# A11·B11 by seven quarter products as well, with partial sums kept in PSUM, one weight buffer for eight sums, and a new order of the groups

## The chip, the cores and the metric

The kernel runs on one core of a Trainium2 chip. The engines that matter are TensorE (PE in the profile; its weight loads are PEld), VectorE (DVE), ScalarE (ACT), GpSimd (POOL) and SyncE (SP), which here only issues DMAs. Each engine works through its own instructions in the order in which they were issued, and waits on semaphores for the others. SBUF is the on-chip memory that all engines use; PSUM holds the results of matmuls in eight banks of 128x512 f32, and here TensorE writes it, ScalarE and VectorE read it. The metric is device time in microseconds (us), the median of the runs shown. The kernel before takes 1509.22 us (three runs, 1507.74 to 1509.64).

## The reference

```python
def reference(x, w):                    # x: 8 x 2048 x 2048, w: 2048 x 2048, f32
    cs = np.cumsum(x, axis=1)
    diff = cs - np.concatenate([zeros, cs[:, :-1, :]], axis=1)
    return np.matmul(diff, w).astype(np.float32)
```

The difference of the running sum is x again, so what is computed is one product of a 16384x2048 matrix by a 2048x2048 matrix.

## The kernel before, in words

**Tiling.** x is cut into 128 row tiles of 128 rows. Tiles 0 to 3 are multiplied in bf16 while w arrives (`plain`). Tiles 4 to 7 are one group (`group_plain`), and the other 120 tiles are 30 groups of four (`group(g, ...)`, g = 8, 12, ..., 124). In a group the code calls the four tiles g, g+1, h = g+2 and h+1; `next_g`, `next_h`, `next_k`, `next_l` are the four tiles of the next group.

**Outer scheme.** w is cut into four blocks B11, B12, B21, B22 of 1024x1024, held in f16. T1 = B12-B11, T2 = B22-T1, T3 = B22-B12 and T4 = B21-T2 are made once. Row tiles g and g+1 give A11, A12 (the two halves of tile g along the contraction) and A21, A22 (those of tile g+1); h and h+1 give a second set. With S1 = A21+A22, S2 = S1-A11, S3 = A11-A21 and S4 = A12-S2, seven products replace eight: A11·B11, A12·B21, S4·B22, A22·T4, S1·T1, S2·T2, S3·T3. The four output blocks C11, C12, C21, C22 are sums of these. A product of one set is 16 matmuls of 128x512; for g and h together 32.

**Inner scheme.** A product for g and h together can itself be cut into quarters (two row tiles, two halves of the contraction, two column halves) and done by seven quarter products of four matmuls each, 28 instead of 32. It needs four sums of x parts (`sums_in`: s1 = a21+a22, s2 = s1-a11, s3 = a11-a21, s4 = a12-s2; VectorE, f16, 128x512 each) and four sums of weight parts (Q1 to Q4 of class `Inner`). The sums of weights are made once where there is room. Where there is not, the sum is made anew in every group into the one buffer `flow` (`passed` in the code): two such sets by GpSimd (`pass_fourth`, line 503), two by VectorE (lines 499 and 815), four instructions of 128x512 f16 a set. From g = 16 on (`five`) the products of A12, S4, A22 and S1 are done by sevens; A11·B11, S2·T2 and S3·T3 are whole. That makes 4x28 + 3x32 = 208 matmuls in a group.

**Evacuation.** Every quarter product ends in a PSUM bank of its own and is then added into the outputs it belongs to, in SBUF. The first part of an output is copied by ScalarE (`keep`, line 543, 16 of 128x512 a group), every other part is added by VectorE (`add`, line 546, out = bank x scale + out, all f32, 36 of 128x512 a group). An output half tile of 128x512 then goes to HBM (`put`, 16 DMAs of 256 KB a group, into seven rotating buffers).

**Input.** For each row tile SP loads two halves of 128x1024 f32 into `F` (`load`), ScalarE sums absolute values row by row (`weigh`, line 112), VectorE and GpSimd make the scale (`scale_of`), ScalarE writes the tile scaled in f16 into the first half's buffer (`narrow`, line 143), and two transposing DMAs bring it to the form that TensorE wants (`turn`). `F` has five half buffers: three for first halves, two for second halves. The transposed tile of the next group goes to the place of the same tile of this group, once that has been read for the last time.

**What sets the order.** Each engine's order is the order in which the code writes the instructions (`after` ties each to the one before on its engine), SP's queue of DMAs included. Nothing is planned by costs. The order of a group is written out by hand in `group`, with two-k steps of S2·T2 and S3·T3 (`go`, four matmuls each) put between the quarter products.

Of the kernel before, what the change touches and what calls it, by code (L numbers as in the profile page):

```python
# [10 lines left out]
def kernel(  # L11
# [51 lines left out]
    F = const.tile([P, 5, NH], f32, name="F")  # L63
# [6 lines left out]

    def bank(i):
        return psum.tile([P, NB], f32, name=f"b{i}")
# [14 lines left out]
    queue_of_x = [PLAIN, PLAIN + 2, PLAIN + 3]  # L87
    for t in range(PLAIN + 4, END, 4):
        queue_of_x += [t, t + 2, t + 1, t + 3]
    for i, t in enumerate(queue_of_x):  # L90
        where[t] = [F[:, i % 3, :], F[:, 3 + i % 2, :]]
# [4 lines left out]
    def load(t, i):  # L96
        if t < END:
            after(
                "sp",
                lambda: nc.sync.dma_start(  # L100
                    where[t][i], x2[ds(t * P, P), ds(i * NH, NH)]
                ),
            )
# [33 lines left out]
    def narrow(t, sides=range(2)):  # L137
        if t < END:
            s = scales[t]
            for i in sides:  # L140
                after(
                    "act",
                    lambda: nc.scalar.activation(  # L143
                        narrowed(t)[:, ds(i * NH, NH)], where[t][i], COPY, scale=s
                    ),
                )

# [3 lines left out]
    def turn(t, halves=range(2)):  # L151
        if t < END:
            for i in halves:
# [5 lines left out]
                )  # L159

    with tc.tile_pool(name="ring", bufs=7) as ring, tc.tile_pool(
        name="o", bufs=5
# [99 lines left out]
        def plain_out(h, r):  # L262
            for n in here(h, r):
                if h == r == 0:
                    c = F[:, 2, ds(n * NB, NB)]
                elif h == 0 or r > 0:
                    c = opool.tile([P, NB], f32, name="o")
                else:
                    c = ring.tile([P, NH], bf16, name="wb").bitcast(f32)
# [167 lines left out]
    class Quarter:  # L437
# [9 lines left out]
    spills = ctx.enter_context(  # L447
        tc.tile_pool(name="spills", bufs=1, space=bass.MemoryType.DRAM)
    )
    inner = inpool.tile([P, 24, NB], f16, name="inner")  # L450
    flow = inpool.tile([P, 4, NB], f16, name="flow")
    spill = [spills.tile([P, 4, NB], f16, name=f"spill{i}") for i in range(4)]
    spare = [inner[:, j, :] for j in range(8, 24)]
    spare += [B12[k][:, n, :] for k in range(KH) for n in range(2)]
    spare += [B22[k][:, 0, :] for k in range(4, 8)]
    spare.reverse()
    S1 = [Part(inner[:, ds(2 * i, 2), :]) for i in range(2)]
    passing = [Quarter(inner[:, j, :]) for j in range(4, 8)]
    free = [cpool.tile([P, NB], f32, name=f"c{i}") for i in range(7)]

    def pair():
        return [one_c() for _ in range(2)]

    def one_c():
        return free.pop(0)


    class Inner:
        def __init__(self, b):
            self.Q1, self.Q2 = ([spare.pop() for _ in range(4)] for _ in range(2))  # L470
            self.Q4 = None
            self.t11, self.t12, self.t21, self.t22 = (
                [t[:, n, :] for t in b[4 * a : 4 * a + 4]] for a in range(2) for n in range(2)
            )
            self.Q3 = self.t12

        def first(self):
            less(self.Q1, self.t12, self.t11)
            less(self.Q2, self.t22, self.Q1)

        def fourth(self):
            if self.Q4 is None:
                self.Q4 = [spare.pop() for _ in range(4)]
            less(self.Q4, self.t21, self.Q2)

        def third(self):
            less(self.t12, self.t22, self.t12)

    passed = [flow[:, k, :] for k in range(4)]

    def keep_flow(i):
        after("sp", lambda: nc.sync.dma_start(spill[i], flow))

    def bring_flow(i):
        after("sp", lambda: nc.sync.dma_start(flow, spill[i]))

    def less(dst, p, q):
        for k in range(len(dst)):
            after("dve", lambda: nc.vector.tensor_tensor(dst[k], p[k], q[k], SUB))  # L499

    def pass_fourth(i):
        for k in range(4):
            after("pool", lambda: nc.gpsimd.tensor_tensor(passed[k], i.t21[k], i.Q2[k], SUB))  # L503

    def total(dst, p, q, op):
        after("dve", lambda: nc.vector.tensor_tensor(dst.all, p.all, q.all, op))  # L506


    def steps(to, a, b, first, pieces):
        for i in range(pieces):  # L510
            ks = range(i * KH // pieces, (i + 1) * KH // pieces)

            def some():
                for k in ks:
                    for n in range(2):
                        said = nc.tensor.matmul(  # L516
                            to[n],
                            a[k],
                            b[k][:, n, :],
                            start=(first and k == 0),  # L520
                            stop=(k == KH - 1),
                            skip_group_check=True,
                        )
                return said

            yield lambda: after("pe", some)

    def product(to, a, b, first):
        for some in steps(to, a, b, first, 4):
            some()  # L530

    def quarter(to, a, b, first):
        def some():
            for k in range(4):
                said = nc.tensor.matmul(  # L535
                    to, a[k], b[k], start=(first and k == 0), stop=(k == 3), skip_group_check=True
# [5 lines left out]
    def keep(c, p, u):  # L542
        after("act", lambda: nc.scalar.activation(c, p, COPY, scale=u))  # L543

    def add(c, p, u):
        after("dve", lambda: nc.vector.scalar_tensor_tensor(c, p, u, c, MUL, ADD))  # L546

    def keeps(c, p, u):
        for n in range(2):
            keep(c[n], p[n], u)  # L550

    def adds(c, p, u):
        for n in range(2):
            add(c[n], p[n], u)

    def put(c, t, at):
        after("sp", lambda: nc.sync.dma_start(out2[ds(t * P, P), ds(at * NB, NB)], c))
        free.append(c)

    store = put  # L560

    def puts(c, t, h):
        for n in range(2):
            put(c[n], t, 2 * h + n)
# [4 lines left out]
    def sums_in(a, b, to):  # L569
        a11, a12, a21, a22 = a.half(0), a.half(1), b.half(0), b.half(1)  # L570
        s1, s2, s3, s4 = to

        def one():
            total(s1, a21, a22, ADD)
            total(s2, s1, a11, SUB)

        def two():
            total(s3, a11, a21, SUB)
            total(s4, a12, s2, SUB)

        return one, two, (a11, a12, a22, s1, s2, s3, s4)


    in_2, in_3 = Inner(B21), Inner(B22)
    in_3.Q4 = [spare.pop() for _ in range(4)]
    in_4, in_5 = Inner(T4), Inner(T1)
    for i in (in_2, in_4, in_5):
        i.Q4 = passed
    assert not spare

    def group_plain(g, X, Y, Z, V):
# [13 lines left out]
        C11g = pair()  # L605
        keeps(C11g, X, ug)
# [4 lines left out]
        adds(C11g, V, ug)  # L611
        puts(C11g, g, 0)
# [6 lines left out]
        C11h = pair()  # L619
        keeps(C11h, Y, uh)  # L620
# [7 lines left out]
        C22 = pair()  # L628
        keeps(C22, V, vg)
        total(S4g, A12g, S2g, SUB)  # L630
        product(X, S2g, T2, False)
        C12g = pair()
        keeps(C12g, X, ug)
# [13 lines left out]
        adds(C11h, Z, uh)  # L647
        puts(C11h, h, 0)
        adds(C12g, V, ug)
        puts(C12g, g, 1)  # L650
        product(Y, S2h, T2, False)
        C12h = pair()
        keeps(C12h, Y, uh)
        adds(C22, X, vg)
        puts(C22, g + 1, 1)
# [5 lines left out]
        C22 = pair()  # L661
        keeps(C22, Z, vh)
# [3 lines left out]
        in_2.first()  # L666
        in_2.fourth()
        load(h + 5, 0)
        load(h + 5, 1)
        keep_flow(0)  # L670
        scale_of(g + 5)
        adds(C22, Y, vh)
        puts(C22, h + 1, 1)
        product(Z, S4h, B22, False)
        in_2.third()
        adds(C12h, Z, uh)
        puts(C12h, h, 1)
        narrow(g + 5)
        turn(h + 4)
        product(X, A22g, T4, False)  # L680
        C21 = pair()
        keeps(C21, X, vg)
        puts(C21, g + 1, 0)
# [3 lines left out]
        in_3.first()  # L687
        in_3.fourth()
        in_3.third()
        product(Y, A22h, T4, False)  # L690
        C21 = pair()
        keeps(C21, Y, vh)
        puts(C21, h + 1, 0)
# [3 lines left out]
        turn(h + 5)  # L697


    def group(g, X, Y, q, e, v, w):  # L700
        h = g + 2
        five = g > PLAIN + 8
# [7 lines left out]
        next_g, next_h, next_k, next_l, then = g + 4, h + 4, g + 5, h + 5, g + 8  # L710
        P6g, P6h = steps(X, S2g, T2, False, 4), steps(Y, S2h, T2, False, 4)
        P7g, P7h = steps(X, S3g, T3, False, 4), steps(Y, S3h, T3, False, 4)

        def go(some, n=1):
            for _ in range(n):
                next(some)()

        def seven(A, Q, Cg, Ch, fill):
            a11, a12, a22, s1, s2, s3, s4 = A
            go(fill)  # L720
            quarter(q, a11, Q.t11, True)
            add(Cg[0], q, ug)
            quarter(e, s1, Q.Q1, True)
            add(Ch[1], e, uh)
            quarter(v, a12, Q.t21, True)
            add(Cg[0], v, ug)
            quarter(q, s2, Q.Q2, False)
            add(Cg[1], q, ug)
            quarter(e, s4, Q.t22, False)
# [281 lines left out]
```

## Time and profile before

| | before |
|---|---|
| median of three runs | 1509.22 us |
| the profiled execution, first to last instruction | 1507.4 us |
| its mean granted TensorE clock | 0.998 |
| one group, from the start of one A11·B11 to the next (1366.32 to 1411.70) | 45.38 us |
| TensorE busy in that group | 45.25 us |
| VectorE busy in that group | 40.97 us |
| ScalarE busy in that group | 26.55 us |
| GpSimd busy in that group | 11.17 us |

Busy times are unions of the instructions' spans, and the spans of neighbouring instructions overlap a little: a 128x512 add is 745 ns long, yet 18 in a row take 12.32 us. Where a price is wanted, the spacing of a row of equal instructions is the better number. "Idle before" is the time in which the engine did nothing before an instruction of the group, with what ended it.

### The profile page before, as it was taken

What the parts mean: (1) busy time and instruction counts of PE and PEld (TensorE: products, weight loads), DVE (VectorE), ACT (ScalarE), POOL (GpSimd) and SP (SyncE); (2) the same over time, 40 slices, a digit from 0 to 9 for tenths busy, and PEclk for the clock granted to TensorE, in tenths of its full rate; (3) what the DMA queues carried; (4) which work ended last, traced back from release to release, by engine and by line L of the source; (5) the groups of instructions that cost most, each with busy time, mean ns of one, the idle gap of its engine ahead of it and who ended that gap; (6) DMA issues with size and microseconds to landing.
All of it is one profiled execution on the core that took longest, in us unless ns stands there. A gap on an engine that the chain in (4) does not pass through costs nothing.

```text
span 1507.4 us, 21215 instructions
## 1 busy us (share of the span) xinstructions
PE 1480.5 (98%) x6799; PEld 661.8 (44%) x6799; DVE 1329.6 (88%) x2419; ACT 914.2 (61%) x1301; POOL 328.9 (22%) x360
## 2 busy tenths in 40 slices
PE   8988999999999999999999999999999999999998
PEld 3433444444444444444444444444444444444443
DVE  7987778889998899998899998999898899888997
ACT  5865656656656656656656656556656556666552
POOL 0100001122221122222122222122222122212222
PEclk9999999999999999999999999999999999999999
DMA  9988979988888988788987888987788988888962
GB/s 359 354 216 243 248 228 249 254 243 211 232 223 229 253 242 212 235 221 233 252 244 205 235 220 240 249 245 205 233 217 244 256 224 219 233 219 241 253 177 105
DMA packets 378912, 354.28 MB, mean 235 GB/s; under 512 B 274928, under 2 KB 275440, under 8 KB 378672
## 3 DMA queue, kind: packets, MB, share of 16 engines
q1 hardware_dynamic: 378240, 351.09, 83.5%
q0 software_dynamic: 560, 1.84, 0.3%
q8 instruction: 53, 0.87, 0.2%
q14 instruction: 59, 0.48, 0.1%
HBM read 151.52 MB, written 136.31 MB: 191 GB/s over the span
## 4 chain that ended last, share of the span: by engine, by line
PE 75%; DVE 13%; issue 4%; DMA 4%; ACT 3%; SPq 0%; DVEq 0%; ACTq 0%
PE b L535 37%; PE b L516 36%; DVE c L546 9%; DVE inner L506 3%; DMA W<-in_w_dram 2%; PE b L250 2%; ACT c L543 1%; DMA x<-F 1%; DVE W L499 1%; DMA W<-in_x_dram 0%; DMA out_dram<-c 0%; DVE x L506 0%; ACT W L361 0%; ACT waste L112 0%; DVE m L129 0%
## 5 line engine op out<-in xcount | busy, mean ns | idle before, releaser
L546 DVE SCALAR_TENSOR_TENSOR c<-b,u,c 128x512 f32<-128x512 f32 x1048 | 736.6, 745 | 125.4 <-PE b L535 81.3
L516 PE MATMUL b<-W,x 128*128 128x512 f16 x3072 | 717.9, 380 | 5.9 <-ACT c L543 3.8
L543 ACT ACTIVATE c<-b,u 128x512 f32<-128x512 f32 x496 | 315.5, 680 | 283.6 <-issue 147.8
L516 PEld LDWEIGHTS <-x 128*128 128x128 f16 x3072 | 300.9, 98 | 370.5 <-issue 8.4
L143 ACT ACTIVATE F<-F,s 128x1024 f16<-128x1024 f32 x246 | 282.4, 1148 | 162.3 <-DVE s L131 158.3
L535 PE MATMUL b<-W,inner 128*128 128x512 f16 x1392 | 338.3, 379 | 0.0
L112 ACT ACTIVATE waste<-F 128x1024 uint8<-128x1024 f32 x246 | 259.5, 1055 | 115.0 <-DMA F<-in_x_dram 110.9
L535 PEld LDWEIGHTS <-inner 128*128 128x128 f16 x1744 | 168.5, 98 | 215.3 <-DVE c L546 15.3
L132 POOL TENSOR_SCALAR u<-m,uw 128x1 f32<-128x1 f32 x124 | 66.6, 542 | 817.0 <-DVE m L129 809.0
L535 PEld LDWEIGHTS <-x 128*128 128x128 f16 x1560 | 152.1, 98 | 195.9 <-issue 14.6
L535 PE MATMUL b<-W,x 128*128 128x512 f16 x968 | 234.2, 379 | 1.5
L503 POOL TENSOR_TENSOR flow<-W 128x512 f16<-128x512 f16 x140 | 163.6, 1195 | 291.2 <-PE b L535 286.8
L506 DVE TENSOR_TENSOR x<-x,x 128x1024 f16<-128x1024 f16 (+1 forms) x214 | 147.2, 700 | 6.2 <-PE b L516 1.1
L503 POOL TENSOR_TENSOR flow<-W,W 128x512 f16<-128x512 f16 x84 | 94.9, 1160 | 0.0
L535 PE MATMUL b<-flow,x 128*128 128x512 f16 x352 | 90.3, 379 | 2.5 <-DVE c L546 2.5
L506 DVE TENSOR_TENSOR inner<-x,x 128x1024 f16<-128x1024 f16 (+1 forms) x122 | 67.4, 553 | 3.3 <-DMA x<-F 3.3
L250 PE MATMUL b<-wb,xP 128*128 128x512 bf16 x240 | 57.4, 393 | 5.0 <-ACT wb L234 3.6
L535 PE MATMUL b<-inner,x 128*128 128x512 f16 x240 | 61.6, 379 | 0.7 <-DVE x L506 0.7
L535 PE MATMUL b<-inner 128*128 128x512 f16 x240 | 61.6, 379 | 0.4 <-DVE c L546 0.4
L506 DVE TENSOR_TENSOR inner<-x,inner 128x512 f16<-128x512 f16 x60 | 51.7, 862 | 0.0
L112 ACT ACTIVATION_READ_ACCUMULATOR waste<-F 128x1 f32 x246 | 46.6, 190 | 0.0
L506 DVE TENSOR_TENSOR x<-inner,x 128x1024 f16<-128x1024 f16 x62 | 42.4, 683 | 3.2
(56 smaller groups left out, 510.2 us busy)
## 6 DMA issues: line engine op xcount, KB each, us to landing
out_dram<-c SPq DMA_DIRECT2D x496, 256.0 KB, 3.2
F<-in_x_dram SPq DMA_DIRECT2D x246, 512.0 KB, 4.9
W<-in_w_dram SPq DMA_DIRECT2D x32, 512.0 KB, 9.6
W<-in_x_dram SPq DMA_DIRECT2D x16, 256.0 KB, 7.7
x<-F SPq DMA_TRANSPOSE x246, 3.4
out_dram<-o SPq DMA_DIRECT2D x7, 256.0 KB, 3.6
spill<-flow SPq DMA_DIRECT2D x3, 512.0 KB, 2.6
out_dram<-o POOLq DMA_DIRECT2D x5, 256.0 KB, 4.2
```

Of the source, the lines that this page charges most:

```text
L112: lambda: nc.scalar.activation(waste, where[t][i], ABS, scale=1.0 / ROW, accum_out=sums_of[t][:, i : i + 1],),
L132: after("pool", lambda: nc.gpsimd.tensor_scalar(u, m, uw, None, MUL))
L143: lambda: nc.scalar.activation(narrowed(t)[:, ds(i * NH, NH)], where[t][i], COPY, scale=s),
L250: lambda: nc.tensor.matmul(ps[r][n], xP[:, r, ko, :], wb[h, ko][:, ds(n * NB, NB)], start=(ko == 0), stop=(ko == KO - 1),),
L499: after("dve", lambda: nc.vector.tensor_tensor(dst[k], p[k], q[k], SUB))
L503: after("pool", lambda: nc.gpsimd.tensor_tensor(passed[k], i.t21[k], i.Q2[k], SUB))
L506: after("dve", lambda: nc.vector.tensor_tensor(dst.all, p.all, q.all, op))
L516: said = nc.tensor.matmul(to[n], a[k], b[k][:, n, :], start=(first and k == 0), stop=(k == KH - 1), skip_group_check=True,)
L535: said = nc.tensor.matmul(to, a[k], b[k], start=(first and k == 0), stop=(k == 3), skip_group_check=True)
L543: after("act", lambda: nc.scalar.activation(c, p, COPY, scale=u))
L546: after("dve", lambda: nc.vector.scalar_tensor_tensor(c, p, u, c, MUL, ADD))
```

## The change

The diff rewrites the groups from g = 8 on; `group_plain` keeps its order. What it does:

- **A11·B11** is done by seven quarter products too, from g = 12 on, and S1·T1 from g = 12 instead of 16. A group then has 5x28 + 2x32 = 204 matmuls. In the group of g = 8 the products of A12 and S4 are done by sevens and the five others whole.
- **Sums in PSUM.** The new class `Quarters` gives a seven-product two pairs of banks, h and g. TensorE writes a11·t11 into h[0]; ScalarE copies that bank into g[0] (`slot`, line 617); TensorE goes on accumulating in both. s1·Q1 goes into h[1]. After s2·Q2 has been accumulated on h[0], ScalarE copies h[0] into one of two SBUF tiles `chain` (`out`, line 605) and VectorE writes h[1] + chain into the bank g[1] (`middle`); after s3·Q3 the same with the result in h[1] (`last`). TensorE then accumulates s4·t22 on g[1]. Four adds (line 510, `add`) bring a seven-product to the outputs, where seven did before.
- **Weight sums.** Eight sets a group pass through `flow`: Q4 and Q1 for A11·B11, t21 for A12·B21, t21 for S1·T1, Q1 and Q3 for S4·B22 and A22·T4 each (`give`). Five sets are made by VectorE and three by GpSimd; GpSimd also makes S1 of h (128x1024). The spills to HBM are gone.
- **Buffers.** `F` has four half buffers, handed out as they come free. The outputs have four buffers of 128x1024, and each goes out in one DMA of 512 KB (8 a group instead of 16).
- **Order.** The order of a group is new on every engine. The seven-products of A11 and A12 are interleaved at its start without any `go` step between them; the last adds of A22·T4 (`tail`) stand in the next group, behind its first two quarter products.

```diff
-    F = const.tile([P, 5, NH], f32, name="F")
+    F = const.tile([P, 4, NH], f32, name="F")
...
+    chain = [inpool.tile([P, NB], f32, name=f"chain{i}") for i in range(2)]
...
+        def give(self, name, engine):
+            p, q, op = {
+                "Q1": ("t22", "Q2", SUB),
+                "t21": ("Q4", "Q2", ADD),
+                "Q4": ("t21", "Q2", SUB),
+                "Q3": ("Q2", "t11", SUB),
+            }[name]
+            for k in range(4):
+                tensor(passed[k], self.b[p][k], self.b[q][k], op, engine)
+            self.b[name] = passed
...
+        def out(self):
+            self.lent = chain[lent[0] % 2]
+            lent[0] += 1
+            after("act", lambda: nc.scalar.copy(self.lent, self.h[0]))
+
+        def middle(self):
+            tensor(self.g[1], self.h[1], self.lent, ADD)
+
+        def last(self):
+            tensor(self.h[1], self.h[1], self.lent, ADD)
+
+        def slot(self, i):
+            h, g, b = self.h, self.g, self.right.b
+            if i == 0:
+                quarter(h[0], self.a11, b["t11"], True)
+                after("act", lambda: nc.scalar.copy(g[0], h[0]))
+            elif i == 1:
+                quarter(h[1], self.s1, b["Q1"], True)
+            elif i == 2:
+                quarter(h[0], self.s2, b["Q2"], False)
+                self.out()
+            elif i == 3:
+                quarter(g[0], self.a12, b["t21"], False)
+            elif i == 4:
+                quarter(h[0], self.s3, b["Q3"], False)
+                self.out()
+            elif i == 5:
+                quarter(g[1], self.s4, b["t22"], False)
+            else:
+                quarter(h[0], self.a22, b["Q4"], False)
...
+        P1.slot(0)
+        P1.slot(1)
+        ready["tail"]()
+        P1.three()
+        weigh(next_g, [0])
+        P2.slot(0)
+        P2.slot(1)
+        total(S1g, A21g, A22g, ADD)
+        P2.three()
+        P1.slot(2)
+        P1.four()
+        P1.middle()
+        total(S3g, A11g, A21g, SUB)
+        P1.slot(3)
...
+        C11g = keep(X, ug, halves=[0])
+        P2.slot(2)
+        weigh(next_g, [1])
+        P2.four()
+        P2.middle()
+        P2.slot(3)
+        scale_of(next_g)
+        total(S1h, A21h, A22h, ADD, "pool")
+        if more:
+            in_1.give("Q4", "dve")
+        add(C11g, P2.g, ug, [0])
+        if not P1.plain:
+            P1.slot(4)
+        narrow(next_g, [0])
+        P1.slot(5)
+        if more:
+            P5 = Quarters(P2.banks, S1g, S1h, in_5, room(at))
...
+        P2.slot(4)
+        keep(X, ug, C11g, [1])
+        narrow(next_g, [1])
+        load(next_k, 0)
+        P2.slot(5)
+        add(C11g, P2.g, ug, [1])
+        put(C11g, g, 0)
+        P5.one()
+        P5.two()
+        total(S2g, S1g, A11g, SUB)
+        P1.last()
+        P1.slot(6)
+        if more:
+            in_5.give("t21", "pool")
+        C11h = keep(Y, uh)
+        P2.slot(6)
...
+        P5.slot(0)
+        P5.slot(1)
...
+        go(2)
+        P5.slot(2)
...
+        P3.slot(0)
+        P3.slot(1)
+        P3.three()
+        if more:
+            P4 = Quarters(P3.banks, A22g, A22h, in_4, room(at))
+            P4.one()
+            P4.two()
...
+        in_3.give("Q3", "pool")
...
+        go(2)
+        P3.slot(2)
...
+        def tail():
+            add(C21h, P4.h, vh, [0])
+            P4.last()
+            add(C21h, P4.h, vh, [1])
+            put(C21h, h + 1, 0)
+            load(h + 8, 1)
+            if next_g < END:
+                in_2.give("t21", "pool")
```

Here P1 to P5 are the products A11·B11, A12·B21, S4·B22, A22·T4 and S1·T1; `slot(i)` issues the quarter product i; `one`, `two`, `three` and `four` make s1 to s4; X and Y are the banks on which A11·B11 stands and S2·T2 and S3·T3 are accumulated. In a full group (g = 12 and on) TensorE's order is 51 steps of four matmuls: P1.0, P1.1, P2.0, P2.1, P1.2, P1.3, P2.2, P2.3, P1.4, P1.5, P2.4, P2.5, P1.6, P2.6, P5.0, P5.1, two go, P5.2, P5.3, go, P5.4, P5.5, two go, P5.6, P3.0, P3.1, two go, P3.2, P3.3, go, P3.4, P3.5, two go, P3.6, P4.0, P4.1, two go, P4.2, P4.3, two go, P4.4, P4.5, two go, P4.6.

## The prediction

> **What bounds the kernel now.** I read the page first, for the busy engines, then the busy times of one group, then the timeline of VectorE and GpSimd in that group, because the change moves work between those two.
>
> ```profile
> span 1507.4 us, 21215 instructions
> ...
> PE 1480.5 (98%) x6799; PEld 661.8 (44%) x6799; DVE 1329.6 (88%) x2419; ACT 914.2 (61%) x1301; POOL 328.9 (22%) x360
> ...
> L546 DVE SCALAR_TENSOR_TENSOR c<-b,u,c 128x512 f32<-128x512 f32 x1048 | 736.6, 745 | 125.4 <-PE b L535 81.3
> L516 PE MATMUL b<-W,x 128*128 128x512 f16 x3072 | 717.9, 380 | 5.9 <-ACT c L543 3.8
> ...
> L503 POOL TENSOR_TENSOR flow<-W 128x512 f16<-128x512 f16 x140 | 163.6, 1195 | 291.2 <-PE b L535 286.8
> ```
>
> TensorE is busy nearly the whole span and VectorE is not far behind. The windows view of one full group shows how close:
>
> ```profile
> core 0: us, PE busy (x) PEld busy (x) DVE busy (x) ACT busy (x) POOL busy (x), PEclk, DMA share, GB/s
> 1366.32:1411.70 45.38, 45.25 (x210) 20.27 (x208) 40.97 (x76) 26.55 (x39) 11.17 (x12) 1.00 0.84 226
> ```
>
> Of 45.38 us TensorE is idle for 0.13: it is the bound. 208 matmuls stand in a group; 32 in a row take 6.91 us (1366.16 to 1373.07), 0.216 us each, so 208 need 44.9 us. VectorE has 4.4 us to spare, GpSimd 34, ScalarE 19. The timeline of the same group, whole first and then VectorE alone, shows what VectorE's instructions take:
>
> ```profile
> 1390.80 4.68 POOL L503 TENSOR_TENSOR flow<-W 128x512 f16<-128x512 f16 x4 [4.42 <-PE b L535]
> ...
> 1393.06 1.40 DVE L506 TENSOR_TENSOR x<-x,x 128x512 f16<-128x512 f16 x1
> ...
> 1394.39 1.37 DVE L506 TENSOR_TENSOR inner<-x,inner 128x512 f16<-128x512 f16 x1
> ```
>
> ```profile
> 1368.12 1.42 DVE L499 TENSOR_TENSOR flow<-W,inner 128x512 f16<-128x512 f16 x4
> 1369.46 0.42 DVE L506 TENSOR_TENSOR inner<-x 128x512 f16<-128x512 f16 x1
> 1369.91 0.42 DVE L506 TENSOR_TENSOR inner<-inner,x 128x512 f16<-128x512 f16 x1
> ...
> 1396.00 12.32 DVE L546 SCALAR_TENSOR_TENSOR c<-b,u,c 128x512 f32<-128x512 f32 x18
> ```
>
> This is the reading that decides the forecast. An f16 sum of 128x512 is 0.42 us long, and 1.40 and 1.37 us while GpSimd works on its own row of f16 sums (1390.80 to 1395.48): VectorE waits until the GpSimd instruction in progress ends. The 18 f32 adds from 1396.00 on keep a spacing of 0.685 us ((12.32 - 0.745) / 17), although GpSimd works on four more sums from 1401.41 to 1405.91. So f16 sums of the two engines exclude each other, and f32 adds that read PSUM are free of it. Before, only two VectorE sums a group fall into a row of GpSimd's.
>
> **The change part by part.** All prices per full group.
>
> *TensorE.* 204 matmuls instead of 208: 204 x 0.216 = 44.06 us, 0.86 less. Over the kernel 116 fewer matmuls, 25 us. A matmul onto a bank that ScalarE or VectorE wrote has no row of its own; I price it as any other.
>
> *VectorE's own work.* 36 adds become 20: 20 x 0.685 = 13.7. New are 10 sums PSUM + SBUF to PSUM in f32. No row shows one; the f16 sum's spacing (1.42 us for four, 0.335) is the lower end, the add's length (0.745) the upper; I take the add's spacing 0.685, as the nearest (f32, one PSUM input, same size): 6.9. [...] f16 sums of 128x512: 5 products x 4 of x and 5 sets x 4 of weights are 40; 35 x 0.335 = 11.7 and 5 that need the one just before 5 x 0.45 (1369.46 to 1369.91) = 2.3. Seven of 128x1024 x 0.61 (eight of T1 are 4.9 us busy) = 4.3. Four scales x 0.32 = 1.3. Sum 40.2, against 40.97 busy before: VectorE gets hardly lighter.
>
> *GpSimd.* Three rows of four f16 sums instead of two (1.13 each, 4.6 us a row, some 0.2 longer for each VectorE sum let in between), and S1 of h, 128x1024, no row: one sum's 1.13 is the lower end, three the upper, I take two, 2.3. Together 16 of 44 us, in which a VectorE f16 sum must wait.
>
> *What the exclusion costs.* I follow VectorE's queue through a group, 0 being the start of P1.0; a step of four matmuls is 0.864, VectorE starts 0.2 us after the step it waits for, and TensorE 0.1 after VectorE.
> 1. The adds of C22 and the tail keep VectorE until 3.5. GpSimd makes t21 for A12·B21 from 1.3 (after the first matmul of P1.1) to 6.1. P1.three and S1g fall into it, each to the end of a GpSimd sum: P1.four ends at 7.25 instead of 5.1. Cost 2.1. P1.middle follows at 7.95, and P1.5 wants it at 7.8.
> 2. After the scale of the next tile (9.9) GpSimd starts S1 of h, 10.1 to 12.4. The four sums Q4 for P1.6 stand there: the first ends at 10.2, the others wait, the last ends at 13.35. Cost 2.2. P1.6, due at 10.4, ends at 13.6.
> 3. GpSimd's t21 for S1·T1 follows at once, 12.5 to 17.3. VectorE's two adds pass (14.7), then P5.one, P5.two and S2g go one per GpSimd sum, to 17.9. Cost 2.2. The first go step waits for S2g: TensorE idles from 16.3 to 18.0.
> 4. Then 22 instructions without GpSimd, 11.0 us by the prices above: 28.9. GpSimd's Q3 for S4·B22 starts behind P3.1, 27.5 to 32.6: P3.three, P4.one and P4.two, 32.8. Cost 2.8.
> 5. The remaining work runs free to 51.0; VectorE was at 1.5 in this group's terms when it began, so it comes round after 49.5.
>
> So 40.2 + 2.1 + 2.2 + 2.2 + 2.8 = 49.5 us, with next to no idle time left on VectorE: it becomes the bound, and TensorE (44.06) idles 5.4 a group. Ends: if every blocked sum falls where VectorE would idle anyway, the cost is nothing; if VectorE keeps besides all the 4.4 us idle that it has before, 53.9.
>
> *ScalarE.* 15 copies more x 0.55 (L270, same size, is 0.60 long; L543's spacing is 0.6): 8.3, so 26.6 (29.1 in the next group) become 35 to 37 of 49.5. Not a bound, but the copies that TensorE waits for now stand behind `weigh` (1.25 us) and `narrow` (1.15), which wait for loads and scales. P5.2's copy stands behind the two `weigh` of next_h; TensorE needs it two steps and a go later, 2.6 us. Covered while loads are in time; without that cover each copy costs TensorE what the load is late.
>
> *SP and DMA.* 8 puts of 512 KB for 16 of 256 KB, no spills; the same bytes (0.84 of the DMA time before). With four half buffers the first half of next_l waits for the second transpose of next_g (behind P3.3, step 32): 28.5 + 3.4 + 4.9 (medians to landing) = 36.8 against its `weigh` behind step 40 (34.6). 2.2 us late at TensorE's own pace, nothing at 49.5. All on SP's one queue: a put waits for VectorE, and the loads queued behind it wait along.
>
> *Elsewhere.* g = 8: 216 matmuls for 212, +0.9; its VectorE has 40 extra weight sums (13.4) but some 12 us less of the others, 42, under TensorE's 46.7. `group_plain` and the start keep their order: 0.
>
> Sum against the profiled execution: 1507.4 + 29 x (49.5 - 45.38) + 0.9 = 1507.4 + 119.5 + 0.9 = 1627.8; the median of the runs lies 1.8 above that execution's span: 1630.
>
> **The rivals.**
> *TensorE stays the bound (faster).* Its place is VectorE's slack: as long as blocked time and idle time together stay under 44.06 - 40.2 = 3.9 us, the group is 44.06 plus today's 0.45 of wait, 44.5. 1509.2 + 29 x (44.5 - 45.38) + 0.9 = 1485. For it: before, VectorE's 40.97 fits beside 99.7% of TensorE. Against: two blocked sums cost 2 us there, and four rows of GpSimd's meet f16 work here.
> *VectorE gets in first.* [...] Both rows here show a GpSimd row that was running first; none shows a run of VectorE sums under way. As a mechanism of this kernel: a run of sums spaced 0.335 leaves GpSimd no gap, VectorE loses only about half (4.6), and what is left is 40.2 + 4.6 plus handoffs of 0.7 to 2.7: 45.5 to 47.5, middle 46.5: 1509.2 + 29 x 1.1 + 0.9 = 1542. For it: GpSimd's wait between rows (286.8 us) makes late rows cheap until TensorE needs them. Against: t21 for A12·B21 is due at step 8 (6.05 to 6.9) and ends at 6.1 undelayed.
> *Loads come late.* Loads on four buffers hold up `weigh`, and with it the copies that TensorE waits for: 53 a group, 1509.2 + 29 x 7.6 + 0.9 = 1731. Also here: a gap of TensorE of 3.4 us halves its clock for as long again (115.6 to 119.0 idle, then PEclk 0.56), 1.7 us a time; my longest gap is 2.2.
> That matmuls are not saved is no rival: the program has 116 fewer.
>
> **How the numbers follow.** VectorE bound, 47.5 to 52 a group, 1572 to 1702: 0.57, likeliest 1630. VectorE first, 1514 to 1570: 0.20. TensorE bound: 0.15. Loads late: 0.06. Within 0.2% (about what a measurement can tell from no change): 0.02. The range leaves out the faster case, no change and the top: 1515 to 1690. Faster 0.15, same 0.02, slower 0.83.
>
> **What would show it.** Right: VectorE's busy share of a full group above 95%, f16 sums of 1.3 us or more beside GpSimd's rows and the sums for P1.6 held up by S1 of h, TensorE waiting on sums by VectorE some 5 us a group, clock near 1. Wrong: TensorE busy over 98% in a group (first rival); f16 sums of 0.42 us throughout and longer GpSimd rows (second); `weigh` waiting on loads for microseconds (third). The PSUM sums wrong at 0.4 or above 1 us would move the group by 3 us either way.

## The result, and the profile after

The changed kernel takes 1726.89 us (median of four runs, 1722.57 to 1729.09) against 1508.57 before: 1.1446 times the time, 95% interval 1.1428 to 1.1463. Slower was forecast, at 1630; the time lies above the range given (1515 to 1690).

The page of the changed kernel, the same rows as before (`add` is now line 510 to 512, all sums of VectorE and GpSimd are line 463):

```profile
span 1727.3 us, 21008 instructions
...
PE 1538.1 (89%) x6677; PEld 656.3 (38%) x6683; DVE 1506.6 (87%) x2723; ACT 1148.0 (66%) x1742; POOL 584.2 (34%) x522
...
L476 PE MATMUL b<-W,x 128*128 128x512 f16 x2176 | 556.9, 400 | 53.8 <-DVE x L463 51.6
L495 PE MATMUL b<-W,inner 128*128 128x512 f16 x1698 | 432.6, 385 | 73.6 <-DVE inner L463 51.9
...
L512 DVE SCALAR_TENSOR_TENSOR c<-b,u,c 128x512 f32<-128x512 f32 x612 | 439.8, 745 | 35.6 <-PE b L495 18.1
...
L463 DVE TENSOR_TENSOR b<-b,chain 128x512 f32<-128x512 f32 x294 | 202.9, 690 | 8.3 <-ACT chain L605 8.2
L463 POOL TENSOR_TENSOR flow<-W 128x512 f16<-128x512 f16 x120 | 151.2, 1291 | 139.1 <-PE b L495 139.1
```

TensorE has fewer matmuls and now stands idle for 11% of the span, where before it waited for almost nothing. What it waits for are sums of VectorE. The windows view over 26 full groups (from one S1 of h to the 26th after it) gives the means that the rest of this text uses:

```profile
core 0: us, PE busy (x) PEld busy (x) DVE busy (x) ACT busy (x) POOL busy (x), PEclk, DMA share, GB/s
259.32:1632.66 1373.34, 1229.17 (x5306) 520.75 (x5305) 1208.61 (x2211) 928.44 (x1431) 501.70 (x442) 0.96 0.77 199
```

Divided by 26: a group takes 52.82 us instead of 45.38. TensorE is busy 47.3 and idle 5.5, VectorE busy 46.5 and idle 6.3, ScalarE busy 35.7, GpSimd 19.3. 29 x (52.82 - 45.38) is 215.8 of the 219.9 us between the two spans.

The chain of work that ended last names a resource that it did not name before with such a share, the transposing DMAs (`DMA x<-F`, 11%; before, 0.8%):

```profile
PE 35%; DVE 31%; DMA 18%; issue 6%; ACT 5%; POOL 3%; SPq 2%; POOLq 0%; ACTq 0%; DVEq 0%
PE b L495 19%; PE b L476 14%; DVE inner L463 12%; DMA x<-F 11%; DVE c L512 7%; DVE flow L463 4%; DVE x L463 4%; DMA F<-in_x_dram 3%; POOL inner L463 3%; DVE b L463 3%; PE b L257 2%; SPq L160 2%; DVE W L463 1%; ACT F L143 1%; DMA out_dram<-c 1%
```

And the view of waits over the same 26 groups shows some that the forecast's sum did not hold (total us, times, longest):

```profile
ACT waste L112 <- DMA F<-in_x_dram: 121.6, 84, 4.6
...
DVE m L129 <- ACT waste L112: 62.6, 53, 2.4
...
POOL inner L463 <- DMA x<-F: 32.6, 27, 2.3
...
DVE inner L463 <- POOL inner L463: 27.8, 26, 2.2
```

ScalarE waits for loads before it can weigh a tile, VectorE waits for the row sums that ScalarE has not made (2.4 us a group; before, 15.5 us in the whole kernel; below this is called the wait for the maxima, since the scale is made from it), GpSimd's S1 of h waits for the transposes of next_l (1.25 us a group), and VectorE waits for GpSimd's S1 of h (1.07 us a group).

One group in the timeline, SP and ScalarE first:

```profile
1033.46 2.27 SPq L160 DMA_TRANSPOSE x<-F  x1
1041.31 0.34 SPq L100 DMA_DIRECT2D F<-in_x_dram  x1
1041.74 0.38 SPq L518 DMA_DIRECT2D out_dram<-c  x1
1042.21 2.06 SPq L160 DMA_TRANSPOSE x<-F  x1
```

```profile
1045.92 1.06 ACT L112 ACTIVATE waste<-F 128x1024 uint8<-128x1024 f32 x1 [2.97 <-DMA F<-in_x_dram]
```

SP issues the second transpose of next_k at 1033.46 and then nothing until 1041.31. The load of the second half of tile g+8 is next in its queue, and the buffer that the code hands to it (`stage.pop(0)`, the oldest free one) is the one that this transpose still reads. By the view of SP's waits, 5.5 us of that stretch are the wait for the transpose to land; over the 26 groups, SP's loads wait 152.7 us for transposes, 5.9 us a group. Behind the load wait a put and the transposes of next_l. The load lands at 1045.8, and ScalarE has stood idle for it for 2.97 us. Then VectorE and GpSimd:

```profile
1047.10 0.21 DVE L129 TENSOR_SCALAR m<-m 128x1 f32<-128x1 f32 x1 [1.77 <-ACT waste L112]
...
1051.43 2.64 DVE L463 TENSOR_TENSOR inner<-inner 128x512 f16<-128x512 f16 x2 [0.89 <-POOL inner L463]
1054.00 1.63 DVE L463 TENSOR_TENSOR x<-inner,x 128x1024 f16<-128x1024 f16 x1
```

```profile
1049.27 2.13 POOL L463 TENSOR_TENSOR inner<-x,x 128x1024 f16<-128x1024 f16 x1 [1.04 <-DMA x<-F]
1051.36 5.29 POOL L463 TENSOR_TENSOR flow<-W,W 128x512 f16<-128x512 f16 x4
```

```profile
1052.85 1.04 PE L495 MATMUL b<-W,inner 128*128 128x512 f16 x4 [1.74 <-DVE inner L463]
1055.69 0.61 PE L476 MATMUL b<-W,x 128*128 128x512 f16 x1 [1.81 <-DVE x L463]
```

This is the exclusion that was forecast: P5.one, P5.two and S2g take 2.64 and 1.63 us beside GpSimd's row, instead of some 0.8 and 0.69, and TensorE waits for the first and the last of them. Summed over all f16 sums that overlap GpSimd's and are longer than alone (0.42 us for 512, 0.69 for 1024), VectorE is blocked 7.0 us a group.

### The profile page after: what moved, and what is told of

Read it like the earlier page. It is cut to its first block, busy times and chain, and to the rows that moved or that the text cites. A ratio compares the mean times of both kernels' runs of the same rounds, so it can differ in the third digit from the quotient of the medians.

```text
span 1727.3 us, 21008 instructions
## 1 busy us (share of the span) xinstructions
PE 1538.1 (89%) x6677; PEld 656.3 (38%) x6683; DVE 1506.6 (87%) x2723; ACT 1148.0 (66%) x1742; POOL 584.2 (34%) x522
## 4 chain that ended last, share of the span: by engine, by line
PE 35%; DVE 31%; DMA 18%; issue 6%; ACT 5%; POOL 3%; SPq 2%; POOLq 0%; ACTq 0%; DVEq 0%
PE b L495 19%; PE b L476 14%; DVE inner L463 12%; DMA x<-F 11%; DVE c L512 7%; DVE flow L463 4%; DVE x L463 4%; DMA F<-in_x_dram 3%; POOL inner L463 3%; DVE b L463 3%; PE b L257 2%; SPq L160 2%; DVE W L463 1%; ACT F L143 1%; DMA out_dram<-c 1%
## 5 line engine op out<-in xcount | busy, mean ns | idle before, releaser
L476 PE MATMUL b<-W,x 128*128 128x512 f16 x2176 | 556.9, 400 | 53.8 <-DVE x L463 51.6
L512 DVE SCALAR_TENSOR_TENSOR c<-b,u,c 128x512 f32<-128x512 f32 x612 | 439.8, 745 | 35.6 <-PE b L495 18.1
L476 PEld LDWEIGHTS <-x 128*128 128x128 f16 x2176 | 218.1, 101 | 346.3 <-DVE x L463 66.9
L495 PE MATMUL b<-W,x 128*128 128x512 f16 x1060 | 268.2, 380 | 0.7 <-ACT chain L605 0.6
L495 PEld LDWEIGHTS <-x 128*128 128x128 f16 x1416 | 136.7, 98 | 205.8 <-issue 54.9
L605 ACT COPY chain<-b 128x512 f32<-128x512 f32 x294 | 169.7, 577 | 66.2 <-PE b L495 57.5
L463 DVE TENSOR_TENSOR b<-b,chain 128x512 f32<-128x512 f32 x294 | 202.9, 690 | 8.3 <-ACT chain L605 8.2
L495 PE MATMUL b<-flow,inner 128*128 128x512 f16 x704 | 183.4, 383 | 5.4 <-DVE flow L463 4.6
L463 POOL TENSOR_TENSOR flow<-W,inner 128x512 f16<-128x512 f16 x120 | 142.7, 1219 | 86.3 <-PE b L495 86.1
L463 DVE TENSOR_TENSOR flow<-W,W 128x512 f16<-128x512 f16 x352 | 129.7, 425 | 0.0
L463 DVE TENSOR_TENSOR inner<-x,x 128x512 f16<-128x512 f16 (+1 forms) x150 | 99.0, 689 | 35.0 <-PE b L495 32.9
L463 DVE TENSOR_TENSOR inner<-inner 128x512 f16<-128x512 f16 x116 | 98.9, 853 | 32.8 <-POOL inner L463 28.7
```

The lines of the kernel that those rows point to most:

```text
L463: after(engine, lambda: on.tensor_tensor(dst, p, q, op))
L476: said = nc.tensor.matmul(to[n], a[k], b[k][:, n, :], start=(start and k == 0), stop=(k == KH - 1), skip_group_check=True,)
L495: said = nc.tensor.matmul(to, a[k], b[k], start=(start and k == 0), stop=(k == 3), skip_group_check=True)
L512: lambda: nc.vector.scalar_tensor_tensor(c[:, n, :], p[n], u, c[:, n, :], MUL, ADD),
L605: after("act", lambda: nc.scalar.copy(self.lent, self.h[0]))
```

## The experiments

Three theories. **A**: the f16 sums of VectorE and GpSimd exclude each other, and VectorE sets the pace. **B**: loads and transposes come late and hold VectorE and TensorE. **C**: the halved TensorE clock (PEclk 0.96 over the groups), since the 3.2 us that TensorE is busy beyond 44.06 are about the 3.3 that the forecast's 49.5 lacks. The first four runs separate them; the next eight size them. The table has the means of 25 or 26 full groups, us. "Blocked" is the time by which f16 sums of VectorE beside GpSimd's are longer than alone; it counts as busy time.

| kernel | time | group | VectorE busy | of it blocked | VectorE idle | of it for row maxima | TensorE idle |
|---|---|---|---|---|---|---|---|
| changed kernel | 1726.9 | 52.82 | 46.5 | 7.0 | 6.3 | 2.4 | 5.5 |
| GpSimd's rows without a read | 1636.8 | 49.74 | 39.7 | 0.0 | 10.0 | 3.9 | 3.6 |
| other order of buffers | 1689.4 | 51.41 | 47.6 | 8.4 | 3.8 | 1.5 | 5.2 |
| both | 1579.8 | 47.56 | 40.3 | 0.8 | 7.2 | 2.0 | 2.2 |
| eight matmuls more | 1723.4 | 52.51 | 46.7 | 7.3 | 5.8 | 2.5 | 4.4 |
| small loads | 1667.6 | 50.54 | 47.7 | 8.6 | 2.9 | 1.1 | 4.4 |
| small loads, rows without a read | 1546.0 | 46.47 | 41.2 | 1.9 | 5.3 | 1.2 | 1.5 |
| all sums on VectorE, other order of buffers | 1642.5 | 49.80 | 44.2 | 0.0 | 5.6 | 2.1 | 3.9 |
| A11·B11 whole | 1704.8 | 52.48 | 41.4 | 6.7 | 11.1 | 3.5 | 5.1 |
| small loads, GpSimd reads nothing | 1500.0 | 44.92 | 39.4 | 0.0 | 5.5 | 1.1 | 0.3 |
| load behind the transposes | 1767.4 | 54.11 | 48.1 | 8.8 | 6.0 | 4.1 | 6.1 |
| S1 of h on VectorE | 1658.3 | 50.33 | 46.6 | 6.7 | 3.7 | 1.5 | 4.4 |
| less overlap | 1605.6 | 48.45 | 42.9 | 1.6 | 5.6 | 1.1 | 3.1 |

**1. GpSimd's rows without a read.**

```diff
-                tensor(passed[k], self.b[p][k], self.b[q][k], op, engine)
+                if engine == "pool":
+                    after("pool", lambda: nc.gpsimd.memset(passed[k], 0.0))
+                else:
+                    tensor(passed[k], self.b[p][k], self.b[q][k], op, engine)
```

> The changed kernel, but the three weight sums a group that GpSimd makes are replaced by GpSimd writing zeros to the same places (no SBUF read; the sums themselves are left out, so three weight sets are zero). S1 of h stays on GpSimd. Theory A (the f16 sums of the two engines exclude each other, and this sets the pace): VectorE's blocked time falls from 7.0 to about 2 us a group, the group from 52.9 to 48 to 49.5, the whole to 1590 to 1630 us. Theory B (loads and transposes that come late set the pace): VectorE's blocked time falls as well, but its wait for the tile's maxima grows by as much, and the time stays above 1690 us. Theory C (the halved TensorE clock, 3.2 us of extra TensorE time a group): follows A or B, no prediction of its own.

1636.8 us, 1.0858 times before (1.0812 to 1.0903); 90 us less than the changed kernel. In the full groups no f16 sum of VectorE is lengthened any more, although eight a group overlap GpSimd's writing of zeros; so GpSimd at work and writing does not block here (0.0 us a group for 7.0); what the edit takes from its rows is the reading, with the sum. (S1 of h, which GpSimd still reads for, met no f16 sum of VectorE there.) The group is just above A's bounds. VectorE's wait for maxima grew by 1.5 us, the way B said, but far less than the 7.0 that went, and the time fell below B's 1690. Both are at work.

**2. Other order of the staging buffers.**

```diff
-            where.setdefault(t, [None, None])[i] = stage.pop(0)
+            where.setdefault(t, [None, None])[i] = stage.pop(which)
...
-        load(g + 8, 1)
+        load(g + 8, 1, 1)
```

> The changed kernel with two free staging buffers handed out in the other order: the second half of the tile g+8 takes the buffer that narrowing of next_l frees, instead of that which waits for the second transpose of next_k. Theory B: the load goes out some 5 us earlier, VectorE's wait for the maxima (2.4 us a group) falls below 1 and GpSimd's S1 of h no longer waits for the transpose (1.2 us): 2.5 to 4 us a group, 1610 to 1655 us. Theory A: VectorE is held by GpSimd wherever it stands; at most 1 us a group, 1700 us or more.

1689.4 us, 1.1207 (1.1167 to 1.1247), 37 less. Between the two: more than A allowed, less than B promised. The loads' wait for transposes on SP falls from 5.9 to 1.9 us a group and the wait of S1 of h from 1.2 to 0.2, as B said. The wait for maxima falls by 0.9 and not to below 1. VectorE is blocked more instead (8.4 for 7.0): 9.2 of its sums a group are lengthened, 8.3 before.

**3. Both.** The two edits together.

> Both edits together (three weight sums left out as before). A and B both at work: a group of 44.5 to 46.5 us, 1485 to 1545 us, TensorE busy over 95% of a group and no halved clock between groups. If a third cause holds VectorE (its waits on TensorE and ScalarE by order of the queues), the group stays at 47 or more, above 1560 us.

1579.8 us, 1.0480 (1.0412 to 1.0547): 147 less, more than 90 + 37. The group stays at 47.56, which the expectation put down to a third cause. VectorE still waited 2.0 us for maxima there, so the loads had not been mended, only moved; runs 6 and 9 decide.

**4. Eight matmuls more.** The first quarter product of S1·T1 three times.

```diff
+        if not P5.plain:
+            for _ in range(2):
+                quarter(P5.h[0], P5.a11, P5.right.b["t11"], True)
         P5.slot(0)
```

> The changed kernel with the first quarter product of S1.T1 issued three times instead of once (eight matmuls more a group, same results), where TensorE would stand idle for VectorE. This lifts TensorE's busy share in the stretch after which the clock is halved. Theory C (the halved clock costs the 3 us a group that the forecast lacks): the clock stays near 1 in most groups and the time falls by 60 to 90 us, to about 1640 to 1665. Theories A and B (TensorE is not what the group waits for there): the clock rises and the time stays within 15 us of 1727, or rises a little.

1723.4 us, 1.1432 (1.1377 to 1.1487), and the clock at 0.988 (0.960 in the changed kernel). The clock was almost repaired and the time hardly moved: C falls. In the changed kernel the clock is halved behind stretches in which TensorE has little to do (0.51 behind 3.41 us of which it was busy for 1.04; see the last section), and by this run the slow matmuls there only fill a wait.

**5. Small loads.**

```diff
-                    where[t][i], x2[ds(t * P, P), ds(i * NH, NH)]
+                    where[t][i][:, : NH // 4] if t >= PLAIN + 12 else where[t][i],
+                    x2[ds(t * P, P), ds(i * NH, NH // 4 if t >= PLAIN + 12 else NH)],
```

> The changed kernel, but from row tile 16 on each load brings only the first quarter of its columns (128 KB instead of 512 KB; the rest of the buffer keeps old data, so the result is not that of the reference). Everything else waits as before. Theory B (late loads cost VectorE its 2.4 us of waiting for maxima and 1.2 us at S1 of h): group 49 to 50.5, 1615 to 1660 us. Theory A (exclusion alone sets the pace, the loads' waits are slack of VectorE that moves elsewhere): within 1 us of 52.9, above 1690.

1667.6 us, 1.1051 (1.1019 to 1.1083): 59 less, near B's bounds from above. ScalarE's wait for loads is gone (0.03 us a group for 4.7); VectorE is blocked 1.6 us more than in the changed kernel, which takes part of the gain back. The edit does more than shorten the loads: with less traffic the other DMAs land sooner too (medians: transposes 3.6 us for 4.7, puts 3.5 for 5.5), so the gain is that of all DMAs being in time, not of one buffer.

**6. Small loads, and rows without a read.**

> Small loads and GpSimd writing zeros in place of three weight sums, together. VectorE has 39.5 us of work a group and neither cause is left except S1 of h on GpSimd. If exclusion and late loads are all, TensorE is the bound again: 44.3 to 45.5 us a group, 1480 to 1520 us. If the handing over between TensorE, ScalarE and VectorE through PSUM costs something of its own, the group stays at 46 to 47.5, 1530 to 1575.

1546.0 us, 1.0245 (1.0216 to 1.0275): 46.47 a group, in the range that spoke for a price of the handing over. But one blocked place was left, S1 of h on GpSimd, amid VectorE's four sums for P1.6. VectorE's and GpSimd's timeline of that kernel:

```profile
1037.13 0.74 DVE L464 TENSOR_TENSOR flow<-W,inner 128x512 f16<-128x512 f16 x2
1037.79 2.68 DVE L464 TENSOR_TENSOR flow<-W,W 128x512 f16<-128x512 f16 x2
```

```profile
1037.91 2.28 POOL L464 TENSOR_TENSOR inner<-x,x 128x1024 f16<-128x1024 f16 x1
```

The second VectorE row holds two sums: by the single records the first of them still takes 0.42 us and the other 2.35. So three of the four pass, then GpSimd gets in between, although VectorE's run was under way, and the last one waits. This is so in all 28 groups that have these four sums in a row. So a run of VectorE sums doesn't keep GpSimd out, which was what the second rival lived on.

**7. All sums on VectorE**, with the other order of buffers: `"pool"` becomes `"dve"` at the `give` calls (three sets a group), and S1 of h stands ahead of `P5.one()`.

> The changed kernel with the other order of staging buffers and with all sums that GpSimd makes (three weight sets and S1 of h) made by VectorE; results unchanged. VectorE's own work grows by 12 x 0.335 + 0.61 = 4.6 to 44.1 us a group, its blocked time falls to nothing. Theory A: the blocked time of 8.4 us that the kernel with only the other order of buffers has goes, 4.6 come back: group 47 to 48.5, 1555 to 1605 us. Rival (VectorE's work counts, not the blocking): as slow as with GpSimd or slower, 1689 or more.

1642.5 us, 1.0885 (1.0853 to 1.0916): 47 less than with GpSimd and the same buffers (run 2). The rival falls: VectorE's own work grew by 5.0 us a group, and the kernel is faster, since nothing blocks it. It misses A's 1555 to 1605, since VectorE is idle 5.6 a group: 2.1 for maxima and 1.65 for ScalarE's copies; TensorE waits 2.05 us for copies of ScalarE which wait for adds queued late on VectorE.

**8. A11·B11 whole again.** `ready[1]` is always `Whole(ready["xy"], A11g, A11h, B11)`, and the `give` calls of `in_1` and `make_1` are gone.

> The changed kernel with A11.B11 whole again (208 matmuls a group; its four sums of x, two sums in PSUM and eight sums of weights go from VectorE, 5.3 us, and three copies from ScalarE); the four other products by sevens in PSUM and the new order stay. Theory A: VectorE's own work 34.2 plus blocked time of 5 to 7 plus its waits: the group falls by 4 to 6 to 47 to 49 us, 1555 to 1615 us. Theory B (loads set the pace): 51 or more, above 1670. If it falls to 45.4 (1510) the seventh product alone made the loss.

1704.8 us, 1.1298 (1.1237 to 1.1359), group 52.48, where B expected it (51 or more). VectorE is busy 5.1 us less and the group gets 0.3 us shorter: nearly all of it became idle time (11.1 for 6.3). Had VectorE's sum of work set the pace, as the forecast's 40.2 + 9.3 has it, 5 us would have gone. The seventh product is not what made the loss, and A in the form "VectorE is the bound" falls. What remains of A is the blocking on the way from S1 of h to S2 of g: TensorE's two waits there are as they were (1.8 us a group for P5.one's sum and 1.7 for S2 of g; in the changed kernel 1.9 and 1.8).

**9. GpSimd reads nothing**, small loads: run 6 and

```diff
-        total(S1h, A21h, A22h, ADD, "pool")
+        after("pool", lambda: nc.gpsimd.memset(S1h.all, 0.0))
```

> Small loads as before, and GpSimd writes zeros for its three weight sums and for S1 of h too (those sums are left out), so GpSimd reads no tensor of SBUF beside VectorE. Account of the two causes: in the kernel with small loads and S1 of h still summed by GpSimd a group took 46.47 us, with 1.93 us of VectorE blocked by that one sum and TensorE idle 1.16 us at the product whose weights VectorE makes then. If that is all, the group falls by 1.2 to 1.9 to 44.6 to 45.3 us, 1485 to 1515 us; if handing over through PSUM has a price of its own, it stays above 45.8, 1525.

1500.0 us, 0.9952 times before (0.9932 to 0.9971). The windows view over its 25 groups:

```profile
core 0: us, PE busy (x) PEld busy (x) DVE busy (x) ACT busy (x) POOL busy (x), PEclk, DMA share, GB/s
242.81:1365.70 1122.89, 1114.62 (x5102) 496.69 (x5101) 984.29 (x2126) 887.50 (x1375) 221.18 (x426) 1.00 0.62 164
```

44.92 us a group with TensorE busy 99.3% of it. The order of the queues, the PSUM sums, the copies by ScalarE and the one weight buffer all fit beside 204 matmuls. What lies between 52.82 and 44.92 goes with GpSimd's reads and three quarters of the loads' bytes, and handing over through PSUM has no price of its own that could be seen. The run does not say how the 7.9 us divide: with GpSimd's sums went also their length (VectorE's 1.07 us of waiting for S1 of h), and with the loads' bytes the slower landing of the other DMAs.

**10. The load behind the transposes** of next_l on SP's queue, same buffer.

```diff
-        load(g + 8, 1)
...
         turn(next_l, [1])
+        load(g + 8, 1)
```

> The changed kernel with one DMA moved in SP's queue: the load of the second half of tile g+8, which waits for a buffer, stands behind the two transposes of next_l instead of ahead of them; same buffers. Two readings of the gain of the other order of buffers (1727 to 1689): (a) the load held the transposes behind it on SP's queue, and S1 of h and TensorE waited for those: then this gives as much, 1680 to 1700 us, and GpSimd's wait for the transpose goes from 1.2 to below 0.3 us a group; (b) the load itself was late for weighing: then it stays at 1715 or more and VectorE's wait for the maxima stays at 2.4 us or grows.

1767.4 us, 1.1728 (1.1694 to 1.1763): 40 more. GpSimd's wait for the transposes vanishes and VectorE's wait for maxima goes to 4.1 us. It is the load itself that counts most, reading (b); what the transposes' delay costs by itself the run does not show.

**11. S1 of h on VectorE**, with the other order of buffers.

> The changed kernel with the other order of buffers and with S1 of h alone made by VectorE, ahead of the first sum that needs it; results unchanged. Theory A: the 1.9 us that VectorE's weight sums for the last quarter product of A11.B11 are blocked behind it go, 0.6 us of own work come, and GpSimd's next row starts 2 us earlier and so meets less of VectorE's chain to S2 of g: group from 51.4 to 48.5 to 50, 1605 to 1650 us. Rival (the order of the queues, not the blocking, sets the pace): within 0.7 us, 1670 or more.

1658.3 us, 1.1005 (1.0973 to 1.1037), 50.33 a group: 1.1 less than run 2, between A's bound and the rival's. VectorE is still blocked 6.7 us, by the three rows that are left.

**12. Less overlap.** As run 11; t21 for S1·T1 on VectorE too; `P4.one()` and `P4.two()` behind the put of C12 of g; `narrow(next_h)` and `load(next_k, 1)` behind `P5.slot(4)`.

> As the run before, and besides: t21 for S1.T1 on VectorE too, the first two sums of A22.T4 behind GpSimd's remaining row, narrowing of next_h and the load that follows it earlier (behind the copy of the fifth quarter product of S1.T1). Results unchanged. VectorE's own work 41.5 us, blocked 1 to 2. Theory A with late loads: 46.5 to 48.5 us a group, 1545 to 1600 us; not below the kernel before (45.38), since the kernel without either cause still took 46.47. Rival: as slow as with all sums on VectorE, 1640.

1605.6 us, 1.0655 (1.0624 to 1.0686): 6 us above the range expected, with the group at its end (48.45). It is the fastest of the changed kernels that do all the work, 121 less than the changed kernel and 99 more than the one before. Blocked time is 1.6 us. No run points to an order that computes everything and beats the kernel before; a full rewrite of the order wasn't tried.

## Why the prediction was wrong

- **TensorE's 204 matmuls**: right, 5306 in 26 groups. Matmuls onto banks written by other engines cost next to nothing extra: TensorE is busy 0.219 us a matmul in run 9 and was 0.218 before.
- **VectorE's own work, 40.2**: 46.5 busy less 7.0 blocked, 39.5. The ten PSUM sums are 690 ns long, and the next instruction starts some 0.60 us after one; the add's spacing was about 0.8 us a group too much.
- **The exclusion, 9.3**: right in kind, 7.0 in size. S1 of h by GpSimd took 2.13 us (2.3 taken), and the wait of the first go step for S2 of g 1.8 us (1.7 forecast). Against the second rival, GpSimd gets in between the sums of a VectorE run (run 6, where the fourth of four took 2.35 us). Beside GpSimd's writing of zeros no f16 sum was lengthened (runs 1 and 9, blocked 0.0). VectorE's adds took 0.743 us beside GpSimd's sums in the changed kernel and 0.746 alone, as was forecast of them.
- **"With next to no idle time left on VectorE"**: wrong, and the first step that failed. VectorE is idle 6.3 us a group and busy for 88% of it, where the forecast's sign was 95%. That TensorE stands idle some 5 us a group came true (5.5), but not because VectorE has no time left. Its sum of work and blocking doesn't set the pace; taking 5.1 us of work away changed the group by 0.3 (run 8).
- **"SP and DMA ... nothing at 49.5"**: the step that hid the cause. It followed the wait of next_l's first half and did not follow which buffer the load of g+8's second half is given. It is the one that the second transpose of next_k still reads, so SP stands for 5.5 us in the group shown, the weighing is late, the scale holds VectorE's queue, and with it the sums for TensorE. Smaller loads alone are worth 2.3 us a group, rows without a read alone 3.1, both 6.35 and with S1 of h 7.9: together they are worth more than one by one, and a sum of the one without the other had to come out low. The 3.3 us a group that 49.5 lacks, times 29, are about the 97 us between 1630 and 1727. With the loads in time (run 5) the group is 50.54, 1.0 above the forecast, with 2.9 us of VectorE idle. The buffer alone is worth less, 1.4 us (run 2); how much of the rest of run 5's gain is due to the lighter DMA traffic stays open. The forecast had no term for that: it took the landing times of the kernel before (3.4 us for a transpose), and the median is 4.7 now.
- **ScalarE, 35 to 37**: 35.7.
- **The clock**: forecast near 1, measured 0.96, but without a price (run 4).
- **The rivals**: the time is that of the third (53 a group, 1731), which had 0.06 and was left out of the range. Its sign, `weigh` waiting on loads for microseconds, is there (4.7 us a group). That its number fits is luck: no sum led to the 53, late loads alone don't make it (with the loads late and nothing blocked a group took 49.74, run 1), and its path was ScalarE's copies, where the longest waits of TensorE are for VectorE's sums. What spoke for late loads was on the table: four buffers instead of five, loads, transposes and puts on one queue in order. I priced the wait of one load where a group has eight. TensorE as the bound and VectorE getting in first did not come about.

## What to carry to other kernels

Where a buffer is handed out as the oldest free one, write down for each load which instruction frees the buffer that it gets: on SP's one queue here a load that waited for a transpose held everything behind it, 5.5 us in the group shown, and was itself late for whoever waited for it, which cost most here (run 10). Before moving elementwise work to GpSimd, look in the trace for VectorE's instructions beside such work and see whether they are lengthened: in the kernel before, f16 sums of 0.42 us took 1.37 beside GpSimd's sums, and adds of 0.746 us took 0.743. Here it was faster to give all the sums back to VectorE, 5.0 us a group of work more and 1.6 us a group less time. An engine at 87% of the span is not a bound until taking work from it shortens the time.

## What the runs showed of the hardware that was not expected

The TensorE clock was halved in the changed kernel without a long gap. The trace lists the granted clock in pieces of 3.41 us. Windows of the changed kernel on that grid, with the longest single gap of TensorE 1.81 us:

```profile
1048.64:1052.06 3.42, 2.46 (x10) 0.79 (x9) 2.24 (x4) 2.73 (x5) 2.79 (x2) 1.00 1.01 216
1052.06:1055.47 3.41, 1.04 (x4) 0.31 (x4) 3.38 (x3) 0.00 (x0) 3.41 (x4) 1.00 0.96 368
1055.47:1058.88 3.41, 3.19 (x8) 1.19 (x9) 3.31 (x7) 2.55 (x5) 1.18 (x1) 0.51 0.78 317
1058.88:1062.30 3.42, 3.42 (x17) 1.50 (x16) 3.35 (x8) 2.78 (x5) 0.46 (x1) 0.99 0.38 153
```

After a piece in which TensorE is busy 1.04 of 3.41 us (0.30) the clock is 0.51 for one piece; after that piece, busy for 0.93, it is back. Over the whole trace, every piece at full clock with TensorE busy 0.40 or less was followed by half clock (27 pieces, start and end of the program included), and none with 0.47 or more. In the trace of the kernel before, the two pieces with 0.20 and 0.03 were followed by half clock, and none with 0.48 or more. The forecast had looked only for gaps of 3.4 us, like the one in the trace of the kernel before; here a piece in which TensorE was busy for 0.30 was followed by half clock too.
